# A batched matrix multiply on one core: the last input loaded by one DMA, and six small loads put between two stores

## The chip, the cores and the metric

The kernel runs on one core of a Trainium2 chip. The time is device time in microseconds (us) for one execution; most executions of a kernel agree within 0.3%. Positions in a trace are microseconds from the start of the profiled span; the span is about 2 us shorter than the time.

## The reference

```python
# x: [32, 256, 512] float32,  y: [32, 512, 384] float32
def reference(x, y):
    return np.einsum('bij,bjk->bik', x, y).astype(np.float32)
```

## The kernel before

The 32 products are worked through in eight groups of four. A letter and a group number stand for each part of the work: `x`, `y` load, `T` rounds and transposes x (VectorE), `R` rounds y to float16 (VectorE), `M` multiplies (TensorE), `C` and `D` copy the results out of PSUM, the memory that the multiplications write to (ScalarE and VectorE), `S` stores. The plan is the program order on every engine; all DMAs are issued from the sync engine's queue (SP) in this order.

```python
PLAN = """
x0 x1 y0
T0 x2 y1
T1 R0 M0 C0 x3 y2
...                                   # cut: groups 2 to 5 in the same way
T6 D4 R5 M5 C5 y7
T7 D5 R6 M6 C6 R7 M7 C7 D7 S3 S4 S5 S6 S7
"""
...
    x_pool = ctx.enter_context(tc.tile_pool(name="x_pool", bufs=2))
    y_pool = ctx.enter_context(tc.tile_pool(name="y_pool", bufs=2))
...
    def load_y(n):                    # y7 alone goes in four quarters
        y_of[n] = y_pool.tile([P, T, K], F32, name="y_sb")
        src = y[n * Q : (n + 1) * Q].rearrange("g (q t) k -> (g q) t k", t=T)
        step = STEP if n == N - 1 else T
        for a in range(0, T, step):
            keep(nc.sync.dma_start(out=y_of[n][:, a : a + step], in_=src[:, a : a + step]))

    def round_y(n):                   # four casts for each group
        y_sb = y_of.pop(n)
        yr_of[n] = yr_pool.tile([P, T, K], MM_DT, name="y_r")
        for a in range(0, T, STEP):
            keep(nc.vector.tensor_copy(yr_of[n][:, a : a + STEP], y_sb[:, a : a + STEP]))
...
    def store(n):                     # one DMA for groups 0 to 5, two for groups 6 and 7
        ...
        for u in range(Q // per):
            b = n * Q + u * per
            keep(nc.sync.dma_start(
                out=out[b : b + per].rearrange("g (s f) k -> (g s) f k", s=w), in_=o[:, u]))
```

The framework (Tile) places the semaphore waits; the kernel's text has none. Its DMAs signal on eight completion semaphores in turn (eight numbers for the 29 DMAs in the trace of before), and a DMA may have to wait for the last user of its own.

Of the kernel before, what the change touches and what calls it, by code (L numbers as in the profile page):

```python
# [1 line left out]

# [4 lines left out]


MM_DT = mybir.dt.float16
F32 = mybir.dt.float32  # L10
P = 128


Q = 4
STEP = 4
O_BUFS = 5
WIDE_GROUPS = 6




PLAN = """
x0 x1 y0
T0 x2 y1
T1 R0 M0 C0 x3 y2
T2 D0 R1 M1 C1 x4 y3 S0
T3 D1 R2 M2 C2 x5 y4 S1
T4 D2 R3 M3 C3 x6 y5
T5 D3 R4 M4 C4 x7 y6 S2
T6 D4 R5 M5 C5 y7  # L30
T7 D5 R6 M6 C6 R7 M7 C7 D7 S3 S4 S5 S6 S7
"""


@with_exitstack
def kernel(
    ctx: ExitStack,
    tc: tile.TileContext,
    x: bass.AP,
    y: bass.AP,  # L40
    out: bass.AP,
):
    nc = tc.nc

    B, I, J = x.shape
    _, _, K = y.shape

    PQ = P // Q
    R = I // PQ
    T = J // PQ  # L50
    TW = T // 2
    NE = I // P
    N = B // Q

    x_pool = ctx.enter_context(tc.tile_pool(name="x_pool", bufs=2))
    y_pool = ctx.enter_context(tc.tile_pool(name="y_pool", bufs=2))
    xr_pool = ctx.enter_context(tc.tile_pool(name="xr_pool", bufs=1))
    xt_pool = ctx.enter_context(tc.tile_pool(name="xt_pool", bufs=3))
    yr_pool = ctx.enter_context(tc.tile_pool(name="yr_pool", bufs=2))
    o_pool = ctx.enter_context(tc.tile_pool(name="o_pool", bufs=O_BUFS))  # L60
    psum_pool = ctx.enter_context(
        tc.tile_pool(name="psum", bufs=2 * Q, space=bass.MemoryType.PSUM)
    )

    keep = tc.keep_in_program_order




    x_of, y_of, xt_of, yr_of, ps_of, o_of = {}, {}, {}, {}, {}, {}  # L70

    def width(n):
        return PQ if n < WIDE_GROUPS else 2 * PQ

    def on_vector(n, e, g):
        if n < WIDE_GROUPS:
            return (e, g) == (NE - 1, Q - 1)
        return n == N - 1 and g % 2 == 1

    def load_x(n):  # L80
        x_of[n] = x_pool.tile([P, R, J], F32, name="x_sb")
        keep(
            nc.sync.dma_start(  # L83
                out=x_of[n],
                in_=x[n * Q : (n + 1) * Q].rearrange("g (p r) j -> (g p) r j", r=R),
            )
        )

    def load_y(n):
        y_of[n] = y_pool.tile([P, T, K], F32, name="y_sb")  # L90
        src = y[n * Q : (n + 1) * Q].rearrange("g (q t) k -> (g q) t k", t=T)
        step = STEP if n == N - 1 else T
        for a in range(0, T, step):
            keep(nc.sync.dma_start(out=y_of[n][:, a : a + step], in_=src[:, a : a + step]))

    def transpose_x(n):


        x_r = xr_pool.tile([P, R, J], MM_DT, name="x_r")
        keep(nc.vector.tensor_copy(x_r, x_of.pop(n)))  # L100
        xt_of[n] = xt_pool.tile([P, NE, TW, P], F32, name="xt_sb")
        b = width(n) // PQ
        src = x_r.bitcast(F32).rearrange("p (b h e) (q t) -> p b e t h q", b=b, e=NE, t=TW)
        dst = xt_of[n].rearrange("p e t (h s b) -> p b e t h s", s=PQ, b=b)
        for e in range(NE):
            for c in range(b):
                keep(nc.vector.transpose(dst[:, c, e], src[:, c, e]))  # L107

    def round_y(n):
# [5 lines that stand above are left out]
    def multiply(n):  # L115
        xt = xt_of.pop(n).bitcast(MM_DT).rearrange("p e t (m c) -> p e t m c", c=2)
        y_r = yr_of.pop(n)
        o_of[n] = o_pool.tile([P, R, K], F32, name="o_sb")
        for e in range(NE):
            for g in range(Q):  # L120
                ps_of[n, e, g] = psum_pool.tile([P, K], F32, name="o_ps")
            for t in range(T):
                for g in range(Q):
                    s = slice(g * PQ, (g + 1) * PQ)
                    keep(
                        nc.tensor.matmul(  # L126
                            ps_of[n, e, g],
                            xt[s, e, t // 2, :, t % 2],
                            y_r[s, t],
                            start=(t == 0),  # L130
                            stop=(t == T - 1),
                        )
                    )

    def collect(n, vector):
        w = width(n)
        per = P // w
        copy = nc.vector.tensor_copy if vector else nc.scalar.copy
        o = o_of[n].rearrange("p (u f) k -> p u f k", u=Q // per)
        for e in range(NE):  # L140
            for g in range(Q):
                if on_vector(n, e, g) != vector:
                    continue
                ps = ps_of.pop((n, e, g))
                a = g % per * w
                for h in range(per):
                    keep(copy(o[a : a + w, g // per, h * NE + e], ps[h * w : (h + 1) * w]))  # L147

    def store(n):
        w = width(n)  # L150
        per = P // w
        o = o_of.pop(n).rearrange("p (u f) k -> p u f k", u=Q // per)
        for u in range(Q // per):
            b = n * Q + u * per
            keep(
                nc.sync.dma_start(  # L156
                    out=out[b : b + per].rearrange("g (s f) k -> (g s) f k", s=w),
                    in_=o[:, u],
                )
            )  # L160

    parts = {
        "x": load_x,
        "y": load_y,
        "T": transpose_x,
        "R": round_y,
        "M": multiply,
        "C": lambda n: collect(n, False),
        "D": lambda n: collect(n, True),
        "S": store,  # L170
    }
    for step in PLAN.split():
        parts[step[0]](int(step[1:]))


# [1 line left out]
_INS = ['x', 'y']  # L177
_OUTS = [((32, 256, 384), 'float32')]


# [23 lines left out]
```

## Time and profile before

| | before |
|---|---|
| time | 135.2 us (134.78 to 135.62, two runs) |
| span profiled | 133.3 us |
| DMA traffic | 54.53 MB on the SP queue, 97% of its sixteen engines' span |
| busy | DVE 72%, ACT 69%, PE 44% |
| last y7 quarter, S5, S7 land | 113.98, 124.94, 132.26 |

The prediction below shows the lines behind this. A "landing" is when a DMA's completion semaphore has its full count.

### The profile page before, as it was taken

Reading aid. Unit: us, or ns where it says so; the run is one execution under the profiler, and the core shown is the slowest. Engines: PE = TensorE matmul, PEld = TensorE weight load, DVE = VectorE, ACT = ScalarE, POOL = GpSimd, SP = SyncE. Lnnn points to the kernel's source line nnn. Section 1 sums busy time; section 2 is a strip of 40 time slices with the busy share of each in tenths; the row PEclk is TensorE's granted clock in tenths of the full one; section 3 lists DMA queues with packets and bytes.
Section 4 is the critical chain, followed back from the end, with each engine's and each line's share of the span. In section 5 each row is a group of like instructions: output and inputs, shape, how many; then the busy total and the mean of one; then the engine's idle time right before and its main releaser. Section 6 shows DMA issues by size and latency. Waiting matters only on the chain.

```text
span 133.3 us, 2449 instructions
## 1 busy us (share of the span) xinstructions
PE 58.7 (44%) x1024; PEld 35.6 (27%) x1024; DVE 96.3 (72%) x92; ACT 91.5 (69%) x193; POOL 0.2 (0%) x4
## 2 busy tenths in 40 slices
PE   0000004960398039806980079200991398776000
PEld 0000002530255025503450046000560275444000
DVE  0049999699969999999069990999999965255300
ACT  3000000099999999999999997999459999997200
POOL 0000000000000000000000000000000000000000
PEclk9999999998569855995599559955599558999655
DMA  5999999999999999999999999999999999999992
GB/s 103 428 423 438 457 413 423 465 406 423 418 472 428 393 433 430 406 400 449 435 457 392 436 423 452 433 401 452 428 428 389 419 424 443 408 432 425 408 415 107
DMA packets 4187, 54.68 MB, mean 410 GB/s; under 512 B 464, under 2 KB 464, under 8 KB 1488
## 3 DMA queue, kind: packets, MB, share of 16 engines
q1 hardware_dynamic: 4176, 54.53, 97.0%
q8 instruction: 8, 0.13, 0.4%
q14 instruction: 3, 0.02, 0.0%
HBM read 41.94 MB, written 12.58 MB: 409 GB/s over the span
## 4 chain that ended last, share of the span: by engine, by line
DMA 39%; DVE 21%; PE 16%; ACT 15%; issue 1%; DVEq 0%; SPq 0%
DMA x_sb<-in_x_dram 39%; PE o_ps L126 16%; ACT o_sb L147 15%; DVE xt_sb L107 7%; DVE o_sb L147 6%; DVE x_r L100 5%; DVE y_r L113 2%; DVEq L199 0%; SPq L156 0%; DVEq L100 0%; SPq L83 0%
## 5 line engine op out<-in xcount | busy, mean ns | idle before, releaser
L147 ACT COPY o_sb<-o_ps 32x384 f32<-32x384 f32 (+1 forms) x192 | 90.2, 470 | 31.8 <-PE o_ps L126 25.9
L126 PE MATMUL o_ps<-y_r,xt_sb 32*128 32x384 f16 x1024 | 58.7, 389 | 63.5 <-DVE y_r L113 60.7
L126 PEld LDWEIGHTS <-xt_sb 32*128 32x128 f16 x1024 | 35.6, 110 | 86.2 <-issue 54.3
L100 DVE CAST x_r<-x_sb 128x4096 f16<-128x4096 f32 x8 | 18.4, 2294 | 19.0 <-DMA x_sb<-in_x_dram 18.9
L107 DVE STREAM_TRANSPOSE xt_sb<-x_r 128x1024 f32<-128x1024 f32 (+1 forms) x20 | 31.6, 1629 | 0.3
L113 DVE CAST y_r<-y_sb 128x1536 f16<-128x1536 f32 x32 | 28.8, 953 | 3.4 <-DMA y_sb<-in_y_dram 3.2
L147 DVE COPY o_sb<-o_ps 32x384 f32<-32x384 f32 (+1 forms) x32 | 17.8, 556 | 5.4 <-PE o_ps L126 4.9
L147 ACT ACT_TABLE_LOAD x1 | 1.3, 1283 | 0.7 <-PEq L188 0.7
L188 POOL MEMSET const-bfloat16-1.0<- 128x1 bf16 x1 | 0.1, 101 | 0.0
L188 POOL MEMSET const-uint8-127<- 128x1 uint8 x1 | 0.1, 101 | 0.0
L188 POOL MEMSET const-float32-0.0<- 128x1 f32 x1 | 0.1, 98 | 0.2 <-issue 0.2
L188 POOL MEMSET const-float32-1.0<- 128x1 f32 x1 | 0.1, 98 | 0.0
## 6 DMA issues: line engine op xcount, KB each, us to landing
y_sb<-in_y_dram SPq DMA_DIRECT2D x7, 3072.0 KB, 22.9
x_sb<-in_x_dram SPq DMA_DIRECT2D x8, 2048.0 KB, 22.5
out_dram<-o_sb SPq DMA_DIRECT2D x6, 1536.0 KB, 23.0
y_sb<-in_y_dram SPq DMA_DIRECT2D x4, 768.0 KB, 14.8
out_dram<-o_sb SPq DMA_DIRECT2D x4, 768.0 KB, 8.5
```

What stands on the lines that cost most here:

```text
L100: keep(nc.vector.tensor_copy(x_r, x_of.pop(n)))
L107: keep(nc.vector.transpose(dst[:, c, e], src[:, c, e]))
L113: keep(nc.vector.tensor_copy(yr_of[n][:, a : a + STEP], y_sb[:, a : a + STEP]))
L126: nc.tensor.matmul(ps_of[n, e, g], xt[s, e, t // 2, :, t % 2], y_r[s, t], start=(t == 0), stop=(t == T - 1),)
L147: keep(copy(o[a : a + w, g // per, h * NE + e], ps[h * w : (h + 1) * w]))
L188: nc = _bacc.Bacc("TRN2", target_bir_lowering=False, num_devices=1)
```

## The change

The y7 load becomes one DMA like the others, and six small loads of x into a spare tile stand between S5 and S6. Nobody reads the tile, so the result doesn't change. They are to show what a few unneeded transfers at this place cost.

```diff
-T7 D5 R6 M6 C6 R7 M7 C7 D7 S3 S4 S5 S6 S7
+T7 D5 R6 M6 C6 R7 M7 C7 D7 S3 S4 S5 L2 L4 L6 L8 L11 L14 S6 S7
@@ load_y
-        src = y[n * Q : (n + 1) * Q].rearrange("g (q t) k -> (g q) t k", t=T)
-        step = STEP if n == N - 1 else T
-        for a in range(0, T, step):
-            keep(nc.sync.dma_start(out=y_of[n][:, a : a + step], in_=src[:, a : a + step]))
+        keep(
+            nc.sync.dma_start(
+                out=y_of[n],
+                in_=y[n * Q : (n + 1) * Q].rearrange("g (q t) k -> (g q) t k", t=T),
+            )
+        )
@@
+    spare = ctx.enter_context(tc.tile_pool(name="spare", bufs=1)).tile([16, 14 * 16], F32, name="spare")
+
+    def load_spare(n):
+
+        keep(nc.sync.dma_start(out=spare[:n, : 16 * n], in_=x[0, :n, : 16 * n]))
+
     parts = {
+        "L": load_spare,
```

## The prediction

Its sum came to 144.3 us: 144.2 from the terms that stand below, and a last 0.1 us for odd row counts. In the second rival, "at most one round trip" is my estimate; and in the third, its 2.3 us, and with it the 146.3 in the range, is my estimate too. That the load of 2 rows uses two engines was not shown then.

> **What bounds the kernel now.** I read the page's slices first, then its queue table, then the trace by window, then the DMA queue's own waits.
>
> From the page of the kernel before: DMA activity in 40 slices, and the queue table.
> ```profile
> DMA  5999999999999999999999999999999999999992
> ...
> q1 hardware_dynamic: 4176, 54.53, 97.0%
> ...
> HBM read 41.94 MB, written 12.58 MB: 409 GB/s over the span
> ```
> The transfers are the bound from start to end: 54.53 MB in 133.3 us, every inner slice at 9 tenths or more. DVE (72%), ACT (69%) and PE (44%) all have room. So a change counts only by the bytes it adds or by a hole that it makes in this stream. The chain that ended last puts only 39% on DMA, because it follows one release at a time; I rely on the slices instead.
>
> From the window view, three stretches around the last loads and stores: length, busy time of the engines, clock, DMA share, GB/s.
> ```profile
> 95.77:113.98 18.21, 12.65 (x227) 8.48 (x223) 14.94 (x16) 15.51 (x33) 0.00 (x0) 0.78 0.99 418
> 113.98:124.94 10.96, 6.53 (x137) 3.78 (x125) 5.41 (x9) 8.99 (x19) 0.00 (x0) 0.97 1.00 419
> 124.94:132.26 7.32, 0.00 (x0) 0.00 (x0) 0.00 (x0) 0.00 (x0) 0.00 (x0) 0.50 0.80 335
> ```
> I cut at landings read from the trace's semaphore records: the last quarter of y7 lands at 113.98, the store of group 5 (S5) at 124.94, the last half of S7 at 132.26. No engine computes in the last 7.32 us: only S6 and S7 (2 x 1.573 = 3.15 MB) drain. Span end minus last landing is 133.3 - 132.26 = 1.0 us.
>
> From the timeline of the sync engine's queue: start, duration, what was issued (the four quarters of y7; S3 to S7; then the last half of S7 alone).
> ```profile
> 95.77 1.75 SPq L94 DMA_DIRECT2D y_sb<-in_y_dram  x4
> 97.56 27.22 SPq L156 DMA_DIRECT2D out_dram<-o_sb  x7
> ...
> 124.45 0.33 SPq L156 DMA_DIRECT2D out_dram<-o_sb  x1
> ```
> All DMAs go out in program order on one queue. S3 and S4 are issued at 97.6 and 98.1, S5 at 111.5, the halves of S6 at 117.4 and 119.4, those of S7 at 123.3 and 124.45. Each is issued before what stands ahead of it has drained (S5 lands only at 124.94); that is why there is no hole. It is also where one can be made.
>
> From the waits of the DMA queue itself: who waited for what, total us, times, longest.
> ```profile
> SPq L94 <- DMA y_sb<-in_y_dram: 32.9, 6, 10.1
> SPq L94 <- DVE y_r L113: 26.5, 6, 5.0
> ...
> SPq L83 <- DMA x_sb<-in_x_dram: 12.7, 4, 6.4
> ```
> A load into a y buffer waits for the earlier load's landing in that buffer, besides its reader. So the framework orders two DMA writes to the same bytes by a semaphore and not by queue order. This is the line on which the prediction turns.
>
> [...] the first load is issued at 0.73 and its first packet starts at 1.74 (1.0 us), and the last data packet ends at 131.92 while its semaphore lands at 132.26 (0.34 us).
>
> **The change, part by part.**
> y7 in one piece removes three issues: 1.75 us of issuing becomes about 0.33, in a stretch where the engines stand at 0.99, so no gain. It moves the same bytes: quarters landed 1.84 us apart (0.786 MB, 427 GB/s), so the whole lands at about 114.0 as before. What it moves is the cast. Before, DVE took each quarter on arrival, the last at 114.01 for 0.96. Now four casts start at 114.0 and end at 117.8. The multiply of group 7 needs them in turn: its first half ends at about 117.8 + 0.8 = 118.6 instead of 118.27; its second half waits until 119.41 for the copies of group 6 anyway. So at most some 0.4 us on S7's readiness at 124.4, with the queue then still holding S6.
>
> The six loads are 2x32, 4x64, 6x96, 8x128, 11x176 and 14x224 floats: 28 KB in all, 0.07 us at 410 GB/s, nothing. But they all write the corner of the one spare tile, each region containing the one before. By the rule read from the waits, L4 is not issued until L2 has landed, L6 until L4 has, and so on; and S6 stands behind L14 in program order.
>
> Step by step. L2 is issued at about 112, right after S5, but its packets stand behind S5's in the same engines, so it lands with S5 at about 124.9 (up to 2 us sooner if its two engines are the early ones; S5's sixteen landings run from 122.71 to 124.94). Then the queue is empty. One round trip of a small load, an estimate from the trace: 1.0 us issue to packet, about 0.4 for a short packet read with nothing else running (the very first 16 KB packets took 1.1 us against 0.6 under way, so a latency of 0.5), 0.34 for the semaphore, 0.05 for the queue to wake: 1.8 us. L4, L6, L8, L11: 4 x 1.8 = 7.2 us, to 132.1. L14 only has to be issued, about 0.4: 132.5. S6 follows at once, its data long ready: 1.0 to the first packet, 7.3 for S6 and S7 (as 124.94 to 132.26 before), 0.34 to land, 0.2 for a ragged restart: 141.3. With 1.0 at the end the span is 142.3, 9.0 over 133.3. Time: 135.2 + 9.0 = 144.2[...].
>
> **The rivals.**
> First: no order among the six loads, only the rotation of completion semaphores. The issue records use eight in turn (the 1st and 9th DMA share one), and a DMA may wait for the last user of its own. Going from 29 to 32 DMAs shifts that: S6's halves would share with S4 and S5, so the second half would go out only at 124.9. The first half (0.786 MB, 1.84 us) covers its 1.0 us to the first packet. Time: about 135.5. For it: before, the third and fourth y7 quarter carry such a wait. Against it: the waits above show that overwriting is ordered too, and this rival needs that rule to stop inside one tile. I give it 7%.
> Second: the chain holds but is partly hidden, L2 landing at 122.7 and the next loads on engines that are free. [...] at most one round trip is saved: 142.5.
> Third: round trips are longer, 2.3 us each[...]: 4 x 0.5 = 2.0 more, 146.3.
> Fourth: the late y7 cast makes compute the bound. Even 1 us later S7 is ready at 125.5, long before its turn in either story; no effect.
>
> **Range and chances.** The hole is four round trips plus one issue and one restart. With 1.4 to 2.3 us per trip the time runs from 142.7 to 146.3; some margin on both sides gives 142.3 to 147.0. Slower by over 2% means over 137.9, which needs only one or two exposed round trips, so it follows wherever the chain exists: 0.92. Within 2% is the first rival: 0.07. A gain has no mechanism: 0.01.
>
> **What the profile after would show.** The six loads in the queue's timeline, the first just after S5 at about 112, the second not before about 123 and the rest 1.4 to 2.3 us apart; a wait of the queue on the spare tile's DMA, about 12 us for the first and some 7 for the other four together; S6 issued near 132.5 instead of 117.4; two or three slices with the DMA near 0 at about 125 to 133; the same 7.3 us for S6 and S7; y7 casts back to back from 114 with no DMA wait between. The prediction is wrong if the six loads go out within 3 us of each other, if a round trip is under 1.2 us or over 2.5, or if S7's copies end after its turn in the queue.

## The result

The changed kernel takes 141.56 us (141.37 to 141.74, two runs) against 135.2: ratio 1.0468, with a 95% interval of 1.0424 to 1.0512. A ratio here is the mean time of one kernel's fast runs over that of the other's fast runs of the same rounds, so not quite the ratio of the medians. The loss was foreseen, its size was not: 6.4 us where 9.1 were forecast, and the time lies below the range (142.3 to 147.0).

The page of the changed kernel: the row of DMA activity and the queue table as in the prediction, and the row of GB/s between them (a slice is now 3.49 us):

```profile
DMA  5999999999999999899999999999999999920596
GB/s 122 423 432 451 444 401 427 455 441 394 439 444 409 430 432 430 367 438 451 434 406 437 432 451 434 390 448 441 403 423 454 419 407 424 419 118 4 241 410 254
...
q1 hardware_dynamic: 3834, 54.56, 92.5%
```

The row of GB/s of the kernel before:

```profile
GB/s 103 428 423 438 457 413 423 465 406 423 418 472 428 393 433 430 406 400 449 435 457 392 436 423 452 433 401 452 428 428 389 419 424 443 408 432 425 408 415 107
```

There is the hole: slices 36 to 38 (122 to 133 us) fall to 118, 4 and 241 GB/s, where the kernel before kept over 400 in its slices 34 to 39. The bytes are nearly the same, 54.56 MB against 54.53.

The window view of the changed kernel, cut at the landing of y7, the landing of S5 and the issue of S6, and ending just before S7's last landing (columns as in the prediction: window, length, busy time of the five engines, clock, DMA share, GB/s):

```profile
114.13:125.08 10.95, 6.19 (x128) 3.69 (x128) 8.01 (x12) 8.67 (x19) 0.00 (x0) 1.00 0.82 345
125.08:129.76 4.68, 0.00 (x0) 0.00 (x0) 0.00 (x0) 0.00 (x0) 0.00 (x0) 0.71 0.01 3
129.76:138.66 8.90, 0.00 (x0) 0.00 (x0) 0.00 (x0) 0.00 (x0) 0.00 (x0) 0.50 0.87 355
```

S5 lands at 125.08, as before (124.94). Then nothing moves for 4.68 us but a few KB, and no engine computes. The first packet of S6 starts at 130.63 by the packet records, and S7 lands at 138.75. From S5's landing to S7's it is 13.67 us in place of 7.32; the difference, 6.35 us, is the whole growth of the span (139.6 - 133.3 = 6.3).

The timeline of the SP queue, changed kernel, in narrow windows (start, duration): the six loads and then the first half of S6.

```profile
111.73 0.59 SPq L169 DMA_DIRECT2D spare<-in_x_dram  x1
...
123.94 0.27 SPq L169 DMA_DIRECT2D spare<-in_x_dram  x1
...
125.25 0.27 SPq L169 DMA_DIRECT2D spare<-in_x_dram  x1
...
126.69 0.27 SPq L169 DMA_DIRECT2D spare<-in_x_dram  x1
...
127.99 0.29 SPq L169 DMA_DIRECT2D spare<-in_x_dram  x1
...
129.36 0.32 SPq L169 DMA_DIRECT2D spare<-in_x_dram  x1
...
129.76 0.37 SPq L159 DMA_DIRECT2D out_dram<-o_sb  x1
```

The issues come one by one, each a round trip after the one before. The waits of the queue (total, times, longest) name what it waits for:

```profile
SPq L169 <- DMA spare<-in_x_dram: 15.6, 5, 11.5
```

Five loads wait for the load before them: 11.5 us for the first, which had stood in its engines behind S5, and 4.1 us in all for the other four. S6's data had long been ready: in the changed kernel's timelines the last copies of all, group 7's, end at 123.8 on ScalarE and 124.2 on VectorE.

### The profile page after: what moved, and what is told of

Read it like the earlier page. It is cut to its first block, busy times and chain, and to the rows that moved or that the text cites. A ratio compares the mean times of both kernels' runs of the same rounds, so it can differ in the third digit from the quotient of the medians.

```text
span 139.6 us, 2457 instructions
## 1 busy us (share of the span) xinstructions
PE 57.4 (41%) x1024; PEld 33.8 (24%) x1024; DVE 96.1 (69%) x92; ACT 91.7 (66%) x193; POOL 0.2 (0%) x4
## 3 DMA queue, kind: packets, MB, share of 16 engines
q1 hardware_dynamic: 3834, 54.56, 92.5%
## 4 chain that ended last, share of the span: by engine, by line
DMA 54%; DVE 17%; PE 11%; ACT 5%; issue 1%; DVEq 0%
DMA x_sb<-in_x_dram 54%; PE o_ps L129 11%; DVE x_r L103 7%; ACT o_sb L150 5%; DVE o_sb L150 4%; DVE xt_sb L110 4%; DVE y_r L116 1%; DVEq L209 0%; DVEq L103 0%; DVEq L150 0%
## 5 line engine op out<-in xcount | busy, mean ns | idle before, releaser
L129 PE MATMUL o_ps<-y_r,xt_sb 32*128 32x384 f16 x1024 | 57.4, 383 | 64.5 <-DVE y_r L116 61.7
L129 PEld LDWEIGHTS <-xt_sb 32*128 32x128 f16 x1024 | 33.8, 109 | 87.8 <-issue 56.7
```

Of the source, the lines that this page charges most:

```text
L129: nc.tensor.matmul(ps_of[n, e, g], xt[s, e, t // 2, :, t % 2], y_r[s, t], start=(t == 0), stop=(t == T - 1),)
```

## The experiments

The theory was this: the framework orders the six overwriting loads by completion semaphores, so S6 stands behind a chain of round trips on an empty queue, and that is all of the 6.4 us. The rivals were that y7 in one piece carries a part, that the loads' mere presence or the rotation of the eight semaphores does, and, for the miss in size, either the first landing or the round trip. All results are right against the reference. The time before in these three calls was 135.38, 135.46 and 135.29 us (medians of 7 to 11 runs).

| run | time, us | ratio to before (95%) | S6 issued at |
|---|---|---|---|
| changed kernel | 141.56 | 1.0468 (1.0424 to 1.0512) | 129.76 |
| e1 y7 in one DMA alone | 135.16 | 0.9991 (0.9973 to 1.0008) | 118.32 |
| e2 six loads alone | 142.17 | 1.0508 (1.0485 to 1.0531) | 130.05 |
| e3 six loads, no overwriting | 134.91 | 0.9972 (0.9951 to 0.9994) | 121.19 |
| e4 six loads in reverse order | 142.71 | 1.0552 (1.0523 to 1.0581) | 131.07 |
| e5 two loads | 136.10 | 1.0061 (1.0044 to 1.0078) | 124.23 |
| e6 twelve loads | 150.00 | 1.1082 (1.1064 to 1.1101) | 138.06 |
| e7 six loads, 16 rows of 8 KB | 148.70 | 1.0984 (1.0964 to 1.1003) | 136.46 |
| e8 six loads on GpSimd's queue | 135.13 | 0.9975 (0.9961 to 0.9988) | 117.62 |
| e9 as e7, rows spread out | 147.68 | 1.0915 (1.0893 to 1.0936) | 135.84 |
| e10 as e7, 128 rows of 1 KB | 145.37 | 1.0746 (1.0717 to 1.0775) | 133.32 |
| e11 six loads after S7 | 140.96 | 1.0414 (1.0388 to 1.0440) | 118.26 |

### The two parts apart (e1, e2)

e1 takes the changed kernel and drops the loads:

```diff
-... S3 S4 S5 L2 L4 L6 L8 L11 L14 S6 S7
+... S3 S4 S5 S6 S7
```

> The last y in one DMA, no extra loads. Theory: the transfers are the bound and y7 lands at the same moment, so 135.2 us, within 0.5% of before; the four casts run back to back from about 114.1 and the last copy of group 7 ends within 0.5 us of 124.4. Rival (the late cast makes the end later and so carries part of the 6.4 us): 136 to 138 us.

Measured: 135.16 us, the same. The timeline of VectorE in e1:

```profile
114.01 3.57 DVE L116 CAST y_r<-y_sb 128x1536 f16<-128x1536 f32 x4 [5.87 <-DMA y_sb<-in_y_dram]
...
123.00 2.28 DVE L150 COPY o_sb<-o_ps 64x384 f32<-64x384 f32 x4 [1.61 <-PE o_ps L129]
```

The four casts run as one block once the whole y7 is there. The last copy ends at 125.28, 0.9 us after that of before, more than I had allowed; but S5 had already been issued 0.9 us later in this run (112.41 against 111.53), before y7 landed, and in the changed kernel, which also loads y7 in one piece, the last copy ends at 124.20. So the shift is not y7's. It costs nothing either way.

e2 is the kernel before, y7 in quarters, with the loads added:

> The kernel before with the six loads between the stores of groups 5 and 6, y7 still in four pieces. Theory: all of the loss is the chain of six loads: 141.6 us, ratio near 1.047, the first small load landing near 124, S6 issued near 130. Rival (y7 in one piece is part of the loss): clearly under 141, for example 139.

Measured: 142.17 us. The loads alone make all of the loss. The time is 0.6 us above that of the changed kernel, but the intervals of the two ratios overlap. In the profiled runs S6 is issued 0.29 us later: the chain starts 0.16 us later (124.10), and one of its four round trips is long, 1.65 us between the loads of 11 and 14 rows, with one landing at 129.63; the three others took 1.26 to 1.33.

### The overwriting, not the loads (e3)

```diff
-    ... .tile([16, 14 * 16], F32, name="spare")
+    ... .tile([16, 45 * 16], F32, name="spare")
+    free = [0]
     def load_spare(n):
-        keep(nc.sync.dma_start(out=spare[:n, : 16 * n], in_=x[0, :n, : 16 * n]))
+        at = free[0]
+        free[0] += 16 * n
+        keep(nc.sync.dma_start(out=spare[:n, at : at + 16 * n], in_=x[0, :n, : 16 * n]))
```

> The changed kernel, but each of the six loads writes columns of its own, so none overwrites another; bytes, number of DMAs and rotation of completion semaphores stay as in the changed kernel. Theory (the overwriting order is the cause): the loads go out without waiting for one another, S6's first half near 121.5 and its second near 125.1 because of the shared completion semaphores, and the time is back at 135.2 to 135.6 us. Rivals: the loads' presence or the rotation of completion semaphores costs the time, then it stays near 141.5.

Measured: 134.91 us. The SP queue's timeline and its waits in e3:

```profile
112.63 5.19 SPq L172 DMA_DIRECT2D spare<-in_x_dram  x6
121.19 5.45 SPq L159 DMA_DIRECT2D out_dram<-o_sb  x4
```

```profile
SPq L159 <- DMA out_dram<-o_sb: 6.5, 2, 3.3
```

All six loads go out in 5.19 us while S3 to S5 still drain. The second line is the prediction's first rival, caught at work: twice a store waits for an older store, since they share a completion semaphore (S6's halves go at 121.19 and 124.83, as S4 and S5 land). It is a real wait and it is hidden: each half is issued while the queue still has something to move (from 124.76 to 132.15 the DMA moves 353 GB/s in e3, against 335 in the last 7.32 us of the kernel before). So overwriting is what makes the loss, not the number of DMAs, their bytes or the rotation.

### The first landing (e4)

```diff
-... S5 L2 L4 L6 L8 L11 L14 S6 S7
+... S5 L14 L11 L8 L6 L4 L2 S6 S7
```

> The changed kernel with the six loads in reverse order (14, 11, 8, 6, 4, 2 rows). Theory: the load of 2 rows came back about 1 us before the last landing of S5, since only its two engines had to be done with S5; with the load of 14 rows first the chain starts only when S5 has landed on nearly all engines, near 125.1, so S6 is issued about 1.2 us later, near 131.0, and the time is 142.7 us. Rival (the first landing doesn't depend on how many engines the load uses): 141.6 us, no change.

Measured: 142.71 us, as expected to 0.01. The first two loads and S6 in e4's timeline:

```profile
112.76 0.73 SPq L169 DMA_DIRECT2D spare<-in_x_dram  x1
...
125.36 0.31 SPq L169 DMA_DIRECT2D spare<-in_x_dram  x1
...
131.07 0.37 SPq L159 DMA_DIRECT2D out_dram<-o_sb  x1
```

With the load of 14 rows in front the chain starts at 125.36 in place of 123.94. In the changed kernel's records each small load has one semaphore update within 0.7 us of its issue and then as many late ones as it has rows: 2, 4, 6, 8, 11 and 14; the store S5, of 128 rows, has sixteen. I read a late landing as one engine; that is an inference from these counts. The load of 2 rows has two packets, at 122.11 and 123.32, and its two late landings are at 122.70 and 123.92, among S5's sixteen, which run from 122.37 to 125.08. So here the load of 2 rows came back 1.16 us before the last part of the store ahead of it had landed.

### How many round trips (e5, e6)

e5 keeps `L2 L14` of the six; e6 has `L2 L3 L4 L5 L6 L7 L8 L9 L10 L11 L12 L14`.

> The changed kernel with two of the six loads, of 2 and of 14 rows. Theory: one wait for a landing near 123.9 and no further round trip, so S6 is issued near 124.35; its first packet follows 0.9 us later, near 125.2, when the slowest engine ended S5 at about 124.8. Nearly all hidden: 136.1 us, ratio 1.006. Rival (every extra load that is waited for costs the same share, a sixth of 6.4 us each): 137.3 us.

> Twelve loads, of 2 to 12 and of 14 rows, in the place of six. Theory: ten round trips stand between the first landing and the issue of S6 in place of four, at 1.36 us each (the mean in the changed kernel): 6 x 1.36 = 8.1 us over the changed kernel, 149.7 us. At the 1.8 us of the prediction it would be 152.4.

Measured: 136.10 and 150.00 us. The SP queue's timeline in e5:

```profile
112.60 11.53 SPq L169 DMA_DIRECT2D spare<-in_x_dram  x2
124.23 3.09 SPq L159 DMA_DIRECT2D out_dram<-o_sb  x4
```

In e5 S6 is issued at 124.23, before S5 has landed (125.15), and nearly all is hidden: 0.6 us is lost (little, but the whole interval of the ratio lies above 1). The four round trips that the changed kernel has besides cost the other 5.5 us (141.56 - 136.10). In e6 the ten trips from 124.05 to 137.70 take 1.25 to 1.53 us, 1.365 in the mean; in the changed kernel four take 1.31, 1.44, 1.30 and 1.36, in the mean 1.355. The waits of the queue in e6:

```profile
SPq L169 <- DMA spare<-in_x_dram: 20.9, 11, 10.5
```

Less the first, 10.4 us of waiting for ten trips; the rest of each is the issue itself, some 0.27 us, and the gap to the next wait.

### Where the chain stands (e8, e11)

e8 issues the loads from GpSimd, on a queue of its own (q0 in its DMA view, 192 packets); e11 puts them behind S7:

```diff
-        keep(nc.sync.dma_start(out=spare[:n, ...
+        keep(nc.gpsimd.dma_start(out=spare[:n, ...
```

```diff
-... S5 L2 L4 L6 L8 L11 L14 S6 S7
+... S5 S6 S7 L2 L4 L6 L8 L11 L14
```

> The changed kernel with the six loads issued from GpSimd's queue and not from the sync engine's; each still waits for the landing of the one before. Theory: the chain costs only where the stores stand behind it in program order; on a queue of its own it runs at the start beside the first loads, S6 is issued near 118 again and the time is 135.2 us, within 0.7%. Rival (chained small loads cost their time wherever they are): 141 us.

> The changed kernel with the six loads after the stores of groups 6 and 7. Theory: S6 is issued near 118 again and S7 lands near 132.3, the load of 2 rows near 131.2, then five round trips of 1.36 us stand alone at the end: last landing near 138.0 and 140.7 us. Rival (the loss is only the stores' late issue): 135.2 to 136 us.

Measured: 135.13 and 140.96 us. In e8 the chain is there and longer, as the waits view shows,

```profile
POOL spare L169 <- DMA spare<-in_x_dram: 28.5, 5, 6.1
```

but no store stands behind it, and it is over by about 41 us, beside the first loads. The SP queue's timeline in e11, from S5 on:

```profile
112.37 13.24 SPq L159 DMA_DIRECT2D out_dram<-o_sb  x5
125.66 11.79 SPq L169 DMA_DIRECT2D spare<-in_x_dram  x6
```

S6 goes out at 118.26 and S7's last landing is at 132.49, 0.2 us later than in the kernel before, but the kernel then waits for the chain alone: the load of 2 rows is issued at 125.66, the other five from 131.34 to 137.14, and the last lands at 138.71. The cost is not the stores' late issue as such; it is time in which nothing runs beside the chain.

### What a round trip depends on (e7, e9, e10)

I had put 0.4 us for reading a short packet into the round trip, taken from 16 KB packets at the kernel's start. e7 was to test whether that was a latency or the packet's length: all six loads become 16 rows of 8 KB. e9 spreads the rows over the partitions, e10 makes them 128 rows of 1 KB.

```diff
-        keep(nc.sync.dma_start(out=spare[:n, : 16 * n], in_=x[0, :n, : 16 * n]))
+ e7:    keep(nc.sync.dma_start(out=spare,      in_=x[0, :64].rearrange("(p r) j -> p (r j)", p=16)))    # [16, 2048]
+ e9:    keep(nc.sync.dma_start(out=spare[::8], in_=x[0, :64].rearrange("(p r) j -> p (r j)", p=16)))    # [128, 2048]
+ e10:   keep(nc.sync.dma_start(out=spare,      in_=x[0, :64].rearrange("a (b j) -> (a b) j", j=256)))   # [128, 256]
```

e9 and e10 were made on e7's miss. My theory for them named a mechanism by which the place of the rows in SBUF counts; no trace or run of this case shows it, so it is cut from both expectations. With it goes a term of 0.63 us of the 1.97 us round trip, and so of the 145.5 us, forecast for e9. The terms of e10 all stand; its 0.31 us is an estimate from 6 KB packets in 0.235 us and takes the 128 KB as spread evenly over sixteen engines.

> Six loads of one size, 16 rows of 8 KB each, overwriting the same bytes. Theory: a round trip is 0.9 us to the first packet, the packet's own time and some 0.35 us to the next issue; an 8 KB packet takes about 0.31 us (6 KB packets take 0.235) where those of up to 896 B take 0.015 to 0.04, so a round trip is about 1.65 us, the first landing near 125.4, S6 issued near 132.4 and the time 144.2 us. Rival (the prediction's 0.4 us is a latency that any read on an idle queue pays, and the small loads escape it for another reason): 2.0 us or more per round trip, over 145.5 us.

> As the run with six loads of 16 rows of 8 KB, but the rows go to partitions 0, 8, 16 and so on in the place of 0 to 15. New theory for that run's miss (2.68 us per round trip where 1.65 was expected): [...] a round trip near 1.97 us, S6 issued near 133.7 and the time 145.5 us. Rival (the cost goes with the 8 KB of a row or with the 128 KB of a load): 2.68 us again and 148.7 us.

> Six overwriting loads of the same 128 KB, as 128 rows of 1 KB. [...] 8 KB per engine take 0.31 us, a round trip near 1.65 us, S6 issued near 132.4 and the time 144.2 us. Rival (the bytes of a load set it): 148.7 us. Rival (eight packets per engine in place of one cost more): over 146 us.

All three missed: 148.70, 147.68 and 145.37 us for 144.2, 145.5 and 144.2. From the packet and issue records, the round trip cut in two:

| | issue to first packet, us | first packet to next issue, us (mean) |
|---|---|---|
| six small loads | 0.88, 0.86, 0.87, 0.89 | 0.48 |
| e10 | about 0.97 | 1.02 |
| e9 | about 1.29 | 1.20 |
| e7 | 0.93 to 1.12 | 1.69 |

An estimate of the second part, the same for all three: 0.45 us, which the small loads take beyond their packets, plus 0.31 for 8 KB at the 26 GB/s that an engine shows (6 KB packets in 0.235 us), 0.76 us. e10 takes 0.26 us more than that, e9 0.44 and e7 0.93. That the place of the rows in SBUF matters is shown: e7 and e9 read the same rows, the second part falls from 1.69 to 1.20 us and the time from 148.70 to 147.68. By what mechanism is not shown, nor what the rest is. Most of e9's miss lies in the first part: its issues take 0.49 us in place of e7's 0.31, and its first packet comes 1.29 us after the issue's start (0.79 after its end) where 0.9 was assumed, 1.6 of the 2.2 us over four trips. For the change it doesn't matter: its own loads have packets of 0.013 to 0.05 us.

## Why the prediction was right or wrong

**The bound and the mechanism: right.** The transfers are the bound; the six loads form a chain by overwriting (e3 against the changed kernel), and S6 waits behind it (its issue follows that of the load of 14 rows at once, and is back at 117.62 when the chain has another queue, e8). The line of waits by which the y loads wait for earlier y loads was the right one to lean on. The main rival, the rotation of semaphores, does exist and is hidden (e3).

**y7 in one piece, no gain and no loss: right** (e1).

**The size: wrong, by two terms of the sum, both too long.**

| step | predicted, us | measured, us | difference |
|---|---|---|---|
| second load issued, the first having landed | 124.9 | 123.94 | -1.0 |
| four round trips | 4 x 1.8 = 7.2 | 5.42 (123.94 to 129.36) | -1.8 |
| issue of the load of 14 rows | 0.4 | 0.40 | 0.0 |
| S6's issue to S7's last landing | 8.84 | 8.99 (129.76 to 138.75) | +0.15 |
| end after the last landing | 1.0 | 0.83 | -0.2 |
| span | 142.34 | 139.57 | -2.8 |

The first step that failed is "it lands with S5 at about 124.9 (up to 2 us sooner if its two engines are the early ones". The spread stood in the landings of the kernel before, and I took its late end for the sum. e4 shows that the order of the loads moves this by 1.2 to 1.4 us. The prediction's second rival was this case, but it undersold it: it held that at most one round trip would be saved, since the next loads would wait for S5 too, and put 142.5 us on it. The load of 4 rows landed at 125.19, 0.11 us after S5, and its round trip, 1.31 us, was no longer than the others (1.30 to 1.44).

The second step that failed is "about 0.4 for a short packet read with nothing else running". The load of 4 rows is issued at 123.94, its packets run from 124.82 to 124.90, its last landing is at 125.19 and the next issue at 125.25: 0.88 + 0.08 + 0.29 + 0.06 = 1.31 us against 1.0 + 0.4 + 0.34 + 0.05. So the packets' term was mis-sized the most, the time to the first packet by 0.12.

That 1.0 us came from the first load of the kernel, whose issue alone takes 0.38 us where the load of 4 rows takes 0.27; from the end of the issue to the first packet both take 0.6 (0.63 and 0.61). So two thirds of this round trip lie before the first packet. The 0.5 us of extra time that I read off the first 16 KB packets is not a toll that every read pays (the first sixteen of them took anything from 0.98 to 2.00 us). e6 fixes the round trip at 1.365 us over ten of them.

Three details were off with little effect. The forecast's last 0.1 us, for odd row counts, doesn't show: in e6 the issues of 3 to 11 rows, odd counts, take 0.26 to 0.29 us, those of 4 to 12 rows, even counts, 0.25 to 0.30. The y7 quarters landed 1.87 us apart and not 1.84. And "some 7" us of waiting for four loads counts whole round trips, though a wait begins only when the issue before it ends (trips of 1.8 us would have shown some 6; it was 4.1). No term of the sum had the issues of the four store halves after the chain: 0.37, 0.38, 0.85 and 1.21 us, against 0.33 each in the kernel before; from S6's issue to S7's last landing the sum was still only 0.15 us short.

**The range: wrong.** It let the round trip vary from 1.4 to 2.3 us, which leaves the measured 1.36 just outside, and kept the first landing fixed. Both errors lay on the same side, so together they left the range; four trips of 1.36 with the landing at 124.9 would still have given 142.5.

## What to carry to other kernels

In this framework a DMA that overwrites what another has just written waited for its landing even on the same queue (five waits, 15.6 us), and everything behind it in that queue waited too (S6 was issued at 129.76 in place of 117.42); give such loads separate bytes (e3, 134.91 us), or a queue with nothing behind them (e8, 135.13 us). On a queue that must never run dry, count the dependent issues that can fall between two large transfers: here the first was nearly hidden behind what was still draining (0.6 us in e5), and each further one cost a full round trip, some 1.36 us. When a round trip goes into a sum, take it from a transfer of the same size and shape (1.36 us for the small loads, 2.68 for 16 rows of 8 KB in e7), and ask which part of the transfer ahead it has to wait for (the chain started at 123.94 behind the load of 2 rows and at 125.36 behind that of 14, e4).
